# A retention and sparse-attention block on one core: the issue order of the second feed-forward's side work

## The chip, the core and the metric

The kernel runs on one core of a Trainium2 chip. The metric is the device time of one execution in microseconds (us), the median of the runs shown. The profile is one further execution, taken by the hardware profiler. PE is the matrix engine, PEld its weight loads, DVE the vector engine, ACT the scalar engine, POOL the general-purpose engine and SP the engine that only issues transfers; a "q" behind a name (SPq, ACTq) means the engine's instruction queue.

## The reference, cut to what matters

The block is a first feed-forward, a mixer (retention and index-selected attention) and a second feed-forward, then a final norm. The change touches only the last two lines:

```python
h = h + 0.5 * swiglu(rmsnorm(h, ffn1_norm), ...)
h = h + hybrid_mixer(rmsnorm(h, mix_norm), ...)
h = h + 0.5 * swiglu(rmsnorm(h, ffn2_norm), ffn2_w_gate, ffn2_w_up, ffn2_w_down)
y = rmsnorm(h, final_norm)          # [512 tokens, 1024], float32
# swiglu(u, wg, wu, wd) = (silu(u @ wg) * (u @ wu)) @ wd, with 2816 features
```

## The kernel before, in words

**Products of split numbers.** PE multiplies in a reduced float32 form. To keep float32 accuracy each operand is split in a high part (ACT copies it to the reduced type) and a low part (DVE subtracts the high part from the original): `in_two`, L323 for the high part and L324 for the low part. A product is then three matmuls, high·high, high·low and low·high. So every weight block costs ACT one high part and DVE one low part before PE can use it. `split` (L117, L118) does the same outside the step list.

**The step list.** The second feed-forward is a list of steps, walked by the generator `steps_through` (L328). Step i does, in program order: the loads of step i+4 (`pre`); the high part of the weights of step i+3 (two steps ahead at the very end); half of its own matmuls; then `lowers()`, the low part of those weights, and `catch_up()`, which runs whatever the list `late` holds; the other half of its matmuls; then its `posts`, side work for ACT and DVE. There are four weight buffers, so the high part of step i+3 has to wait until PE has left step i-1.

**The units.** The 2816 features come in six units, u0 to u5: u0 has 256 features, the others 512. u0 is computed plainly (`Plain`, four steps). Units u1 to u5 (`Rows`) use a seven-product scheme on halves of the tokens and of the inputs: 14 steps of 12 matmuls each (L2317), with sums and differences of weight quarters made by DVE (`wsum`, L2239). Three PSUM results X, Z, Y are made in turn; X lies in one PSUM area, Z and Y share another. ACT copies a result out (`copy`, L2258), DVE adds a second result to it (`add`, L2261), ACT takes silu of it (`silu`, L2266), DVE multiplies gate and up (`gated`, L2270) and turns the block for the next product (`turn`, L2277), POOL writes it to DRAM (`hts`, L2280), SP fetches it back in the other layout (`fetch`, L2287, one per token half: the half of room C first, then that of room D), and ACT and DVE split it again (`hidden`, the features hh and hl that the down product uses as stationary operand).

**Which side work goes where** is written out by hand in `posts_of` (L2560). For units u2 to u5: at step 3 `add("A", "Z")` and at once the silu of A; at step 11 `add("B", "Y")` and at once the silu of B; at steps 12 and 13 the two `gated` and `turn`. Since Y takes the PSUM area of Z, PE's step 6 has to wait for the add of Z at step 3. Since the next unit's X takes the area of X, its step 0 has to wait for `gated` of A.

**The down products** of the unit before (`down`, L2491, four steps of 24 matmuls, L2478) are woven in behind steps 7, 9, 11 and 13 of a unit (8 and 13 in u5). They are (output half c, features k0) = (0,0), (0,2), (1,0), (1,2). After the second step of a half, DVE adds its four PSUM blocks to the residual: `take`, put on `late`, so that it runs in the middle of the next step. For half c = 1 this next step is step 0 of the following unit. The adds are L2471 (four instructions), and L2464 for u0 (16 small ones a half).

**The end.** Behind u5's steps come u4's last two down steps, then u5's down for c = 0 in two steps (features 0 to 1 and 2 to 3, for token blocks b = 0, 1, 2, 3 in this order), then u5's c = 1 outside the step list, with the final norm (`finish`, `leave`). Token blocks 2 and 3 need half 1 of u5's features (room C), blocks 0 and 1 half 0 (room D). The weights of u5's c = 1 are one load of 1 MB (`load_w`, L133) into a buffer that held earlier down weights, split at L117 and L118. The gain of the final norm is loaded by ACT's queue at L2654.

**Who orders what.** Inside `manual_schedule(engines=BUSY)` PE, ACT and DVE issue in the order of the program; SP and POOL, and everything outside, are placed by the framework's planner, which fills a queue by its own estimate of what is ready when. All steps up to u4's second down step are in one such region, the last four steps in a second. Each engine's queue is strictly in order: an instruction that waits holds up those behind it.

Of the kernel before, what the change touches and what calls it, by code (L numbers as in the profile page):

```python
# [11 lines left out]
F32 = mybir.dt.float32  # L12
# [6 lines left out]
P = 128  # L19
D = 1024  # L20
KD = D // P
S = 512
# [59 lines left out]
def kernel(ctx: ExitStack, tc: tile.TileContext, x, meta, g1, wg1, wu1, wd1, gm,  # L82
                      w_in, w_ro, w_ao, w_mo, g2, wg2, wu2, wd2, gf, rope, decay, causal, out):
    nc = tc.nc
# [45 lines left out]
    def load_w(src, nk, n):  # L130
        raw = wpool.tile([P, 2048], F32, tag="raw", name="raw", bufs=2)
        v = raw[:, : nk * n].rearrange("p (k c) -> p k c", k=nk)
        nc.sync.dma_start(v, src.rearrange("(k p) c -> p k c", p=P))  # L133
        return v

    def split_w(v, eng=nc.vector):
        nk, n = v.shape[1], v.shape[2]
        hi = wpool.tile([P, 1024 + WPAD], F32R, tag="whi", name="whi", bufs=3)[:, w_at[0] :]
        lo = wpool.tile([P, 1024 + WPAD], F32R, tag="wlo", name="wlo", bufs=3)[:, w_at[0] :]
        hv = hi[:, : nk * n].rearrange("p (k c) -> p k c", k=nk)  # L140
        lv = lo[:, : nk * n].rearrange("p (k c) -> p k c", k=nk)
        split(v, hv, lv, eng)
        return hv, lv
# [226 lines left out]
    class Sevens:  # L370
# [50 lines left out]
        def gate_of(self, src, t, norm):  # L421

            nc.vector.tensor_tensor(t, src, norm, ALU.mult)
            nc.scalar.activation(t, t, AF.Silu)
            nc.vector.tensor_tensor(t, t, norm, ALU.mult)
            return t
# [23 lines left out]
        def split_t(self, n):  # L450
            split(self.ts[n], *self.tsum(n))
# [135 lines left out]
    if True:  # L587
# [120 lines left out]
        with tc.manual_schedule(engines={mybir.EngineType.PE, mybir.EngineType.Activation, mybir.EngineType.DVE}):  # L708
# [51 lines left out]
            def second_half(k):  # L760

                taken(second[k], 0)
                kept(second[k], False)
# [97 lines left out]
        def down(f0, nf, taken_by):  # L861

            raws = {}
            steps = []
            for c in range(KD):
                def pre(c=c):
                    if c % 2 == 0:
                        raws[c] = load_w(wd1[f0 * P : (f0 + nf) * P, c * P : (c + 2) * P], nf, 2 * P)

                def src(c=c):  # L870
                    return raws[c // 2 * 2][:, :, c % 2 * P : (c % 2 + 1) * P]

                def run(w, lower, c=c):
                    ps = [s1.bank("psd")[:, :TH] for _ in range(2)]
                    mm3([(ps[0], one), (ps[1], two)], w, lambda k: s1.hid[f0 + k], nf)
                    lower()
                    s1.catch_up()
                    for p_, sl in zip(ps, (one, two)):
                        nc.vector.scalar_tensor_tensor(hT[c][:, sl], p_, 0.5, hT[c][:, sl], ALU.mult, ALU.add)
                    taken_by(c)  # L880
                    s1.next_sum4()

                steps.append((pre, src, run))
            return steps
# [522 lines left out]
    if True:  # L1407
# [418 lines left out]
        p = RH - 1  # L1826
# [349 lines left out]
    TT, STT = nc.vector.tensor_tensor, nc.vector.scalar_tensor_tensor  # L2176
    xn = [hidp.tile([P, 4, S], F32, tag=f"h{c}", name="xn") for c in "hl"]
    one, two = slice(0, S // 2), slice(S // 2, S)
    late, f2 = [], {}

    def catch_up():

# [240 lines left out]
    def token_norm():  # L2423
        nc.vector.tensor_scalar(tok[:, 8:12], tok[:, :4], 1.0 / D, EPS, ALU.mult, ALU.add)
        nc.gpsimd.tensor_tensor(rcol, tok[:, 8:12], mhalf[:, :4], ALU.pow)

    def fetch_tokens():
        for b in range(4):
            nc.gpsimd.dma_start(hTok[b], hx[b * P : (b + 1) * P].rearrange("t h a e -> t (h a e)"))
# [58 lines left out]
            banks += [t[:, :S], t[:, S:]]  # L2488
        return banks

    def down(u, c, k0, banks, first=True, last=True, posts=(), taken_by=None, where=("d0", "d1"), held_last=False):  # L2491

        d = {}

        def pre():
            held = last_raw if held_last else down_raw
            if not held:
                t = wpool.tile([P, 2048], F32, tag="raw", name="raw", bufs=2).rearrange("p (h k c) -> p h k c", h=2, k=2)
                held.extend(t[:, i] for i in range(2))
            held.append(held.pop(0))  # L2500
            d["raw"] = held[-1]
            rows = slice((u.f0 + k0) * P, (u.f0 + k0 + 2) * P)
            nc.sync.dma_start(d["raw"], wd2[rows, c * S : (c + 1) * S].rearrange("(k p) c -> p k c", p=P))

        def run(w, lower):
            if k0 == 0 and first:
                banks.extend(new_down(where))
            for b in range(4):
                for k in range(2):
                    products([(banks[b], wide)], u, b, k0 + k, w, k, first and k0 + k == 0, last and k0 + k == u.nf - 1)  # L2510
                if b == 1:
                    lower()
                    catch_up()
            for do in posts:
                do()
            if last and k0 == u.nf - 2:
                def take():
                    for b in range(4):
                        add_sums(b, c, banks[b])
                        if taken_by:  # L2520
                            taken_by(b, c)
                if taken_by:
                    take()
                else:
                    late.append(take)

        return (pre, lambda: d["raw"], run, 0)

    fin = {}

    def finish(b, c):

# [27 lines left out]
    def posts_of(u):  # L2560

        i = u.i
        nxt = units[i + 1] if i + 1 < len(units) else None
        prev = units[i - 1] if i else None
        at = {j: [] for j in range(14)}

        def put(j, *do):
            at[j] += do

        gate_of = lambda c, half: lambda: u.silu(c, half)  # L2570
        if u is u0:
            put(0, lambda: split_t(1), lambda: new_t(2))
            put(1, lambda: split_t(2), lambda: new_t(3), lambda: squares(0))
            put(2, lambda: split_t(3), lambda: new_t(4), lambda: squares(1), lambda: squares(2), lambda: squares(3), token_norm)
            put(3, lambda: split_t(4), u.gates, lambda: u1.wsum(2, 0), lambda: late.append(u.turned))
            return at
        a, b = (4, 6) if u.early else (2, 4)
        put(a, lambda: prev.new_hidden(hid_tile), lambda: late.append(prev.hidden(1)))
        put(1, lambda: u.copy("A", "p1", "X"), lambda: u.wsum(2, 2))
        put(3, lambda: u.add("A", "Z"), gate_of("A", 0))  # L2580
        put(b, lambda: late.append(prev.hidden(0)))
        if not u.early:
            put(4, lambda: u.wsum(3, 0))
            put(5, lambda: u.wsum(3, 2))
        put(5, lambda: u.copy("B", "u2", "X"))
        put(6, lambda: u.wsum(4, 0))
        put(7, lambda: u.copy("C", "p5", "Y"), lambda: u.wsum(4, 2))
        put(9, lambda: u.add("C", "X"))
        put(11, lambda: u.add("B", "Y"), gate_of("B", 1))
        loads = {6: "21", 7: "11", 9: "12", 11: "22"}  # L2590
        put(12, lambda: u.gated("C", u.room["C"], u.room["B"], 1), lambda: u.turn("C", "D", 1), lambda: u.fetch("C", 1))
        put(13, lambda: u.gated("A", u.d["X"], u.room["A"], 0), lambda: late.append(turn_rest))

        def turn_rest():
            u.turn("A", "B", 0)
            u.fetch("D", 0)

        if nxt:
            for j, n in loads.items():
                put(j, lambda n=n: nxt.load(n))  # L2600
        return at
# [7 lines left out]
    def woven(i, places_):  # L2609

        for j, s in enumerate(wo[i]):
            steps.append(s)
            if j in places_:
                steps.append(places_[j])

    def downs(u, posts, **kw):
        banks = ([], [])
        return [down(u, c, k0, banks[c], posts=p, held_last=bool(kw and c and k0), **(kw if c else {}))
                for (c, k0), p in zip([(c, k0) for c in range(2) for k0 in range(0, u.nf, 2)], posts)]

    woven(1, dict(zip((9, 13), downs(u0, ((), sums_of(units[2]))))))
# [1 line left out]
        woven(i, dict(zip((7, 9, 11, 13), downs(units[i - 1], ((), (), (), sums_of(units[i + 1]))))))  # L2623
    u4, u5 = units[4:]

    def second_half():
        u5.new_hidden(last_tile)
        late.append(u5.hidden(1))

    d = downs(u4, ((), (), (second_half,), (lambda: u5.hidden(0)(),)), where=("x", "z"))  # L2630
    woven(5, {8: d[0], 13: d[1]})
    n_units = len(steps)
    c0, c1 = [], []
    steps += d[2:]
    steps.append(down(u5, 0, 0, c0, held_last=True))
    steps.append(down(u5, 0, 2, c0, taken_by=finish))
    pair = []

# [11 lines left out]
            next(pipe)  # L2650
    f2["later"].close()
    fp = fin["p"] = ctx.enter_context(pool("f2"))
    fin["gfb"] = fp.tile([P, D], F32, tag="gfb", name="gfb")
    nc.scalar.dma_start(fin["gfb"], gf.partition_broadcast(P))  # L2654
    fin["sums"] = fp.tile([P, 4, 16], F32, tag="sums", name="sums")
    fin["hg"] = [fp.tile([P, D], F32, tag=f"hg{b}", name=f"hg{b}") for b in range(4)]
    with tc.manual_schedule(engines=BUSY):
        for _ in pipe:
            pass
    raw = load_w(wd2[u5.f0 * P : (u5.f0 + 4) * P, S:], 4, 512)  # L2660
    ws = [split_w(raw[:, i : i + 2, :]) for i in (0, 2)]
    with tc.manual_schedule(engines=BUSY):
        part = slice(0, S // 2)
        c1 += new_down(("x", "z"))
# [57 lines left out]
```

## Time and profile before

| | |
|---|---|
| median of 3 runs (lowest to highest) | 1507.54 us (1506.84 to 1507.86) |
| the profiled execution: its time, its span | 1508.82 us, 1507.0 us |
| PE busy | 1486.2 us, 99% of the span |
| DVE, ACT, POOL busy | 75%, 47%, 11% |
| mean granted PE clock | 0.994 |
| second feed-forward | from 1150.3 us to the end |

How to read it: PE's busy time is the union of its matmuls, which overlap, so a short stop hides in it; the start times of matmuls in the timeline tell more. In the timeline a row is start, length, engine, line, operation, output<-inputs, count, and in brackets the idle time before it and what ended it. In the view of waits a row is engine, tile and line, what it waited for, and then total us, times and the longest.

### The profile page before, as it was taken

What the parts mean: (1) busy time and instruction counts of PE and PEld (TensorE: products, weight loads), DVE (VectorE), ACT (ScalarE), POOL (GpSimd) and SP (SyncE); (2) the same over time, 40 slices, a digit from 0 to 9 for tenths busy, and PEclk for the clock granted to TensorE, in tenths of its full rate; (3) what the DMA queues carried; (4) which work ended last, traced back from release to release, by engine and by line L of the source; (5) the groups of instructions that cost most, each with busy time, mean ns of one, the idle gap of its engine ahead of it and who ended that gap; (6) DMA issues with size and microseconds to landing.
All of it is one profiled execution on the core that took longest, in us unless ns stands there. A gap on an engine that the chain in (4) does not pass through costs nothing.

```text
span 1507.0 us, 22315 instructions
## 1 busy us (share of the span) xinstructions
PE 1486.2 (99%) x8848; PEld 1314.7 (87%) x8848; DVE 1125.1 (75%) x1715; ACT 714.5 (47%) x1028; POOL 159.8 (11%) x238
## 2 busy tenths in 40 slices
PE   9999999999999999999999999999999999999996
PEld 8999999999988888888898888988888878888875
DVE  4988585776886768678978778777567787876855
ACT  5655263454354444443334447667335634434433
POOL 1000000002111120100000032331003110110110
PEclk9999999999999999999999999999999999999997
DMA  5232333236644445231332335576466334354241
GB/s 170 60 119 90 111 100 113 85 99 187 219 146 171 168 139 166 94 122 60 128 101 72 110 97 167 158 199 186 154 225 201 106 119 167 113 167 146 78 151 59
DMA packets 160857, 200.54 MB, mean 133 GB/s; under 512 B 13680, under 2 KB 117256, under 8 KB 160112
## 3 DMA queue, kind: packets, MB, share of 16 engines
q1 hardware_dynamic: 146992, 162.53, 34.1%
q0 software_dynamic: 10080, 29.75, 6.0%
q10 hardware_dynamic: 3680, 6.84, 1.3%
q8 instruction: 69, 1.13, 0.3%
q14 instruction: 36, 0.29, 0.1%
HBM read 168.91 MB, written 30.16 MB: 132 GB/s over the span
## 4 chain that ended last, share of the span: by engine, by line
PE 90%; DVE 5%; issue 2%; ACT 2%; DMA 1%; POOLq 0%; POOL 0%; SPq 0%; DVEq 0%; ACTq 0%
PE psd L157 8%; PE psqX L157 7%; PE psd L2478 6%; PE psrg L157 6%; PE psro L157 6%; PE psqX L2317 5%; PE psvX L1181 4%; PE psqY L157 3%; PE psrk L157 3%; PE psrq L157 3%; PE psga L157 3%; PE psqY L2317 3%; PE psat L157 3%; PE psmo L157 3%; PE psak L157 3%; PE psaq L157 3%
## 5 line engine op out<-in xcount | busy, mean ns | idle before, releaser
L324 DVE TENSOR_TENSOR wlo<-raw,whi 128x1024 fp32r<-128x1024 f32 (+2 forms) x156 | 174.2, 1120 | 41.3 <-ACT whi L323 41.0
L323 ACT ACTIVATE whi<-raw 128x1024 fp32r<-128x1024 f32 (+2 forms) x156 | 147.6, 949 | 105.0 <-PE psd L157 37.5
L324 DVE TENSOR_TENSOR wlo<-w,whi 128x1024 fp32r<-128x1024 f32 x76 | 92.4, 1218 | 45.3 <-ACT whi L323 45.2
L323 ACT ACTIVATE whi<-w 128x1024 fp32r<-128x1024 f32 x76 | 80.1, 1058 | 97.0 <-PE psd L2478 31.2
L157 PE MATMUL psro<-vo,whi 128*128 128x512 f32 x256 | 78.9, 389 | 0.0
L117 ACT ACTIVATE whi<-raw 128x1024 fp32r<-128x1024 f32 (+1 forms) x44 | 45.4, 1036 | 55.6 <-PE psat L157 17.2
L118 DVE TENSOR_TENSOR wlo<-raw,whi 128x1024 fp32r<-128x1024 f32 (+1 forms) x44 | 53.7, 1220 | 23.6 <-ACT whi L117 23.5
L157 PE MATMUL psd<-hl,whi 128*128 128x264 f32 x352 | 71.2, 284 | 0.0
L157 PE MATMUL psd<-hh,wlo 128*128 128x264 f32 x352 | 70.9, 283 | 0.0
L157 PE MATMUL psd<-hh,whi 128*128 128x264 f32 x352 | 70.6, 282 | 0.0
L2478 PE MATMUL psd<-whi,hh 128*128 128x512 f32 (+1 forms) x148 | 58.2, 393 | 4.4 <-ACT hh L323 4.4
L157 PE MATMUL psqX<-th,whi 128*128 128x264 f32 x216 | 61.1, 283 | 0.0
L157 PE MATMUL psqX<-tl,whi 128*128 128x264 f32 x216 | 61.1, 283 | 0.0
L157 PE MATMUL psqX<-th,wlo 128*128 128x264 f32 x216 | 61.1, 283 | 0.0
L2478 PE MATMUL psd<-whi,hl 128*128 128x512 f32 (+1 forms) x148 | 58.2, 393 | 1.7 <-DVE hl L324 1.7
L2478 PE MATMUL psd<-wlo,hh 128*128 128x512 f32 (+1 forms) x148 | 58.1, 392 | 0.5 <-DVE wlo L324 0.5
L157 PEld LDWEIGHTS psro<-vo,whi 128*128 128x128 f32 x256 | 48.1, 188 | 10.2
L157 PEld LDWEIGHTS psd<-hh,wlo 128*128 128x128 f32 x352 | 54.4, 188 | 0.0
L157 PEld LDWEIGHTS psd<-hh,whi 128*128 128x128 f32 x352 | 54.3, 188 | 0.0
L157 PEld LDWEIGHTS psd<-hl,whi 128*128 128x128 f32 x352 | 53.9, 188 | 0.0
L323 ACT ACTIVATE whi<-wsum 128x1024 fp32r<-128x1024 f32 x36 | 38.1, 1059 | 30.3 <-PE psd L157 14.8
L2280 POOL DMA_DIRECT2D hts<-cross x40 | 25.7, 649 | 249.9 <-DVE cross L2277 249.2
(579 smaller groups left out, 4678.4 us busy)
## 6 DMA issues: line engine op xcount, KB each, us to landing
raw<-in_w_in_dram SPq DMA_DIRECT2D x18, 1024.0 KB, 5.4
raw<-in_w_in_dram SPq DMA_DIRECT2D x33, 512.0 KB, 4.0
raw<-in_ffn_w_down_dram SPq DMA_DIRECT2D x24, 512.0 KB, 3.9
w<-in_w_in_dram SPq DMA_DIRECT2D x24, 512.0 KB, 6.2
raw<-in_ffn_w_up_dram SPq DMA_DIRECT2D x11, 1024.0 KB, 5.1
raw<-in_ffn_w_gate_dram SPq DMA_DIRECT2D x10, 1024.0 KB, 5.1
w<-in_ffn_w_up_dram SPq DMA_DIRECT2D x20, 512.0 KB, 4.2
w<-in_ffn_w_gate_dram SPq DMA_DIRECT2D x20, 512.0 KB, 5.4
```

Source lines behind the costliest of these rows:

```text
L117: nc.scalar.activation(hi, src, AF.Copy)
L118: eng.tensor_tensor(lo, src, hi.bitcast(F32), ALU.subtract)
L157: nc.tensor.matmul(o, a[:, k, :], b[:, sl], start=first and k == 0 and i == 0, stop=last and k == nk - 1 and i == 2, skip_group_check=onto)
L323: nc.scalar.activation(hi, src, AF.Copy)
L324: return lambda: nc.vector.tensor_tensor(lo, src, hi.bitcast(F32), ALU.subtract)
L1181: nc.tensor.matmul(d[bank_][t], a, b[:, k, :], start=not onto and j + k + m == 0, stop=j + k == 3 and m == 2, skip_group_check=onto)
L2280: nc.gpsimd.dma_start(d.rearrange("(b i) a e -> a i b e", i=32)[a], cross[32 * a : 32 * a + 32].rearrange("p b c t -> p b (c t)"))
L2317: nc.tensor.matmul(ps[:, t], a, b[:, k, :], start=not onto and j + k + m == 0, stop=j + k == 3 and m == 2, skip_group_check=onto)
L2478: nc.tensor.matmul(ps, a, m[:, j, cs], start=first and i == 0, stop=last and i == 2)
```

## The change

Seven edits, all in the second feed-forward:

1. The silu of A and of B are no longer issued behind their add in `posts`, but put on `late`: they run in the middle of the next step, behind the high part that this step issues.
2. The adds (`take`) of a unit's half c = 1 go on a list of their own, `put_off`, for u0 to u3, and run in `posts` of step 2 of the next unit instead of the middle of step 0. For u4 they stay on `late`.
3. u5's features: half 1 was split (high part in `posts` of u4's third down step, low part in the middle of the fourth) and half 0 in `posts` of the fourth. Now both high parts and then both low parts stand in `posts` of the fourth (`last_halves`).
4. u5's first down step takes the token blocks in the order 2, 3, 0, 1.
5. The load and the splits of the weights for u5's c = 1 move from behind the step list into `posts` of u5's first down step (`tail_weights`).
6. The second region orders SP as well.
7. The gain of the final norm is loaded by SP during u0's step 3, into a part of `RR` that u0's squares used until then, and not by ACT's queue at the end.

```diff
+    def load_gf():
+        fin["gfb"] = RR[:, :D]
+        nc.sync.dma_start(fin["gfb"], gf.partition_broadcast(P))
...
-    def down(u, c, k0, banks, ..., held_last=False):
+    def down(u, c, k0, banks, ..., held_last=False, put_off=late, rows=range(4)):
...
-            for b in range(4):
+            for i, b in enumerate(rows):
...
-                    late.append(take)
+                    put_off.append(take)
...
-            put(3, lambda: split_t(4), u.gates, lambda: u1.wsum(2, 0), lambda: late.append(u.turned))
+            put(3, load_gf, lambda: split_t(4), u.gates, lambda: u1.wsum(2, 0), lambda: late.append(u.turned))
...
-        put(3, lambda: u.add("A", "Z"), gate_of("A", 0))
+        put(2, lambda: put_off and put_off.pop()())
+        put(3, lambda: u.add("A", "Z"), lambda: late.append(gate_of("A", 0)))
...
-        put(11, lambda: u.add("B", "Y"), gate_of("B", 1))
+        put(11, lambda: u.add("B", "Y"), lambda: late.append(gate_of("B", 1)))
...
+    put_off = []
     def downs(u, posts, **kw):
         banks = ([], [])
+        kw = kw or {"put_off": put_off}
...
-    def second_half():
-        u5.new_hidden(last_tile)
-        late.append(u5.hidden(1))
-    d = downs(u4, ((), (), (second_half,), (lambda: u5.hidden(0)(),)), where=("x", "z"))
+    def last_halves():
+        u5.new_hidden(last_tile)
+        lows = [u5.hidden(half) for half in (1, 0)]
+        for low in lows:
+            low()
+    def tail_weights():
+        raw = load_w(wd2[u5.f0 * P : (u5.f0 + 4) * P, S:], 4, 512)
+        tail_w.extend(split_w(raw[:, i : i + 2, :]) for i in (0, 2))
+    d = downs(u4, ((), (), (), (last_halves,)), where=("x", "z"))
...
-    steps.append(down(u5, 0, 0, c0, held_last=True))
+    steps.append(down(u5, 0, 0, c0, held_last=True, posts=(tail_weights,), rows=(2, 3, 0, 1)))
...
-    fin["gfb"] = fp.tile([P, D], F32, tag="gfb", name="gfb")
-    nc.scalar.dma_start(fin["gfb"], gf.partition_broadcast(P))
...
-    with tc.manual_schedule(engines=BUSY):
+    with tc.manual_schedule(engines=BUSY | {mybir.EngineType.SP}):
         for _ in pipe:
             pass
-    raw = load_w(wd2[u5.f0 * P : (u5.f0 + 4) * P, S:], 4, 512)
-    ws = [split_w(raw[:, i : i + 2, :]) for i in (0, 2)]
+    ws = tail_w
```

More of the change, by code (lines that the diff above doesn't have):

```diff
@@ L2178 @@
     one, two = slice(0, S // 2), slice(S // 2, S)
-    late, f2 = [], {}
+    late, f2, fin = [], {}, {}
     def catch_up():
@@ L2489, in new_down, with down @@
         return banks
-    def down(u, c, k0, banks, first=True, last=True, posts=(), taken_by=None, where=("d0", "d1"), held_last=False):
+    def down(u, c, k0, banks, first=True, last=True, posts=(), taken_by=None, where=("d0", "d1"), held_last=False, put_off=late, rows=range(4)):
         d = {}
@@ L2507, in run @@
                 banks.extend(new_down(where))
-            for b in range(4):
+            for i, b in enumerate(rows):
                 for k in range(2):
                     products([(banks[b], wide)], u, b, k0 + k, w, k, first and k0 + k == 0, last and k0 + k == u.nf - 1)
-                if b == 1:
+                if i == 1:
                     lower()
@@ L2524, in run @@
                 else:
-                    late.append(take)
+                    put_off.append(take)
         return (pre, lambda: d["raw"], run, 0)
-    fin = {}
     def finish(b, c):
@@ L2614, in woven @@
                 steps.append(places_[j])
+    put_off = []
     def downs(u, posts, **kw):
         banks = ([], [])
-        return [down(u, c, k0, banks[c], posts=p, held_last=bool(kw and c and k0), **(kw if c else {}))
+        kw = kw or {"put_off": put_off}
+        return [down(u, c, k0, banks[c], posts=p, held_last=bool("where" in kw and c and k0), **(kw if c else {}))
                 for (c, k0), p in zip([(c, k0) for c in range(2) for k0 in range(0, u.nf, 2)], posts)]
@@ L2624 @@
     u4, u5 = units[4:]
-    def second_half():
+    tail_w = []
+    def last_halves():
         u5.new_hidden(last_tile)
-        late.append(u5.hidden(1))
-    d = downs(u4, ((), (), (second_half,), (lambda: u5.hidden(0)(),)), where=("x", "z"))
+        lows = [u5.hidden(half) for half in (1, 0)]
[5 more added lines that the diff above has]
+    d = downs(u4, ((), (), (), (last_halves,)), where=("x", "z"))
     woven(5, {8: d[0], 13: d[1]})
```

## The prediction

> **What bounds the kernel now.** I read the page first (PE busy 99% of the span), then PE's waits from 1150 us on, where the second feed-forward begins.
>
> ```profile
> PE psd L2478 <- ACT hh L323: 4.4, 1, 4.4
> PE psqY L2317 <- DVE p L2261: 1.8, 1, 1.8
> PE psd L2478 <- DVE hl L324: 1.7, 2, 1.4
> ```
>
> PE bounds the stage; what a reordering can win is what PE loses in a few stops. Busy time hides part of them, so I measured starts in the timeline. Undisturbed, a step of 24 matmuls takes 5.44 us, one matmul 0.227:
>
> ```profile
> 1264.78 5.44 PE psqY L2317 x24
> ```
>
> At the end, the last matmul of u4's fourth down step, the first four of u5's, and the one at which the pace is normal again:
>
> ```profile
> 1466.56 0.39 PE L2478 MATMUL psd<-whi,hl 128*128 128x512 f32 x1
> 1471.32 0.80 PE L2478 MATMUL psd<-whi,hh 128*128 128x512 f32 x1 [4.37 <-ACT hh L323]
> 1471.91 0.63 PE L2478 MATMUL psd<-wlo,hh 128*128 128x512 f32 x1
> 1473.91 0.80 PE L2478 MATMUL psd<-whi,hl 128*128 128x512 f32 x1 [1.36 <-DVE hl L324]
> ...
> 1479.96 0.39 PE L2478 MATMUL psd<-wlo,hh 128*128 128x512 f32 x1
> ```
>
> The third matmul was due at 1466.56 + 3 x 0.227 = 1467.24 and started at 1473.91, 6.67 late. The 14 intervals to 1479.96 took 6.05 instead of 3.17, 2.88 more. Together 9.55 us. The slow matmuls are a clock matter: the view by windows has the granted clock (the number behind POOL's) at 0.83 here.
>
> ```profile
> 1467.00:1498.00 31.00, 25.32 (x106) 20.62 (x107) 18.54 (x30) 10.39 (x19) 1.30 (x2) 0.83 0.07 23
> ```
>
> [...]
>
> In u2 (its first matmul, its step 6, and the step behind the first down step):
>
> ```profile
> 1221.25 0.39 PE L2478 MATMUL psd<-whi,hl 128*128 128x512 f32 x1
> 1222.30 0.47 PE L2317 MATMUL psqX<-whi,xh 128*128 128x512 f32 x1 [0.66 <-DVE p L2270]
> ...
> 1239.55 0.39 PE L2317 MATMUL psqX<-wlo,th 128*128 128x512 f32 x1
> 1241.70 0.47 PE L2317 MATMUL psqY<-wpair,th 128*128 128x512 f32 x1 [1.77 <-DVE p L2261]
> ...
> 1253.73 0.39 PE L2317 MATMUL psqX<-whi,th 128*128 128x512 f32 x1
> ```
>
> From 1221.25 to 1253.73 there are 121 intervals: 27.43 us due, 32.48 taken, 5.05 lost, of which 0.82 at the first stop and 1.92 at the second. Two small stops remain, in u1 (0.2) and in u5 at u4's first down step (0.87 - 0.23 = 0.64, and 0.1 for the next matmul: 0.75).
>
> ```profile
> 1191.43 0.39 PE L2317 MATMUL psqY<-whi,tl 128*128 128x512 f32 x1
> 1191.84 0.50 PE L2317 MATMUL psqY<-wlo,th 128*128 128x512 f32 x1
> ...
> 1430.63 0.39 PE L2478 MATMUL psd<-whi,hh 128*128 128x512 f32 x1
> 1431.50 0.50 PE L2478 MATMUL psd<-wlo,hh 128*128 128x512 f32 x1 [0.48 <-DVE wlo L324]
> ```
>
> So at most 0.2 + 5.05 + 0.75 + 9.55 = 15.55 us can be won. The change removes no instruction from PE, DVE or ACT.
>
> **Silus behind the next high parts.** The cause of the stops in u1, u2 and u5 is one pattern. DVE, the end of u1 and the start of u2, and ACT's silu:
>
> ```profile
> 1211.26 1.22 DVE L324 TENSOR_TENSOR wlo<-raw,whi 128x1024 fp32r<-128x1024 f32 x1
> 1212.39 1.22 DVE L2261 TENSOR_TENSOR u<-psqY,u 128x1024 f32<-128x1024 f32 x1
> 1215.96 1.23 DVE L324 TENSOR_TENSOR wlo<-w,whi 128x1024 fp32r<-128x1024 f32 x1 [2.35 <-ACT whi L323]
> ...
> 1228.93 3.69 DVE L2464 SCALAR_TENSOR_TENSOR hTok<-psd,hTok 128x128 f32<-128x128 f32 x16
> ...
> 1236.08 1.23 DVE L324 TENSOR_TENSOR wlo<-w,whi 128x1024 fp32r<-128x1024 f32 x1 [1.19 <-ACT whi L323]
> ...
> 1240.34 1.22 DVE L2261 TENSOR_TENSOR p<-psqZ,p 128x1024 f32<-128x1024 f32 x1
> ```
> ```profile
> 1213.64 1.34 ACT L2266 ACTIVATE u<-u,RR 128x512 f32<-128x512 f32 x2 [4.73 <-DVE u L2261]
> ```
>
> The add releases the silu; the next high part stands behind the silu on ACT, and DVE idles 2.35 us for it. With the change that high part (whose buffer PE has left by then) is done while ACT waited anyway, and DVE goes on at 1212.39 + 1.13 = 1213.5. What waits for the silu itself, `gated`, comes one instruction later, at 1214.65, with the first silu done by 1214.36 and the second by 1214.98: no new wait over 0.3. Behind the silu on ACT now stands only what stood behind that high part. So DVE is 2.4 us earlier at every silu. In u1 that exceeds the 0.2 lost, and in u5 the 0.64: both stops go. At the start of u2, `gated` of A, whose end let PE go at 1222.30, is done by 1219.9, ahead of 1221.25 + 0.23 = 1221.48 where PE wants X: 0.9 goes.
>
> **Adds two steps later.** In u2, DVE reaches the place of the adds at 1228.93 - 2.4 = 1226.5. Now come the low part of step 4 (1.3 with its high part, which needs the sum just made), a weight sum (1.13), the 1.19 of waiting for that sum's high part, the low part of step 5 (1.13): 1231.2. Then the adds (3.7): 1234.9, a low part and half 1's low part (2 x 1.13), the add of Z (1.22): 1238.4, and 0.14 later PE's step 6 (before: 1241.56 to 1241.70). PE wants it at 1221.48 + 6 x 2.72 = 1237.8. So 0.7 remains, 0.8 with the restart: 4.25 of 5.05 is won. Between the ends (DVE not ahead at all: 2 us stay; the adds fill every wait: 0) I take the sum. The features' low part for half 0 is ready 0.2 before PE's third down matmul; if not, 0.3 is lost.
>
> In u3 to u5 nothing waited at Z. u5's adds and its add of Z, and PE's step 6:
>
> ```profile
> 1409.48 2.47 DVE L2471 SCALAR_TENSOR_TENSOR hTok<-psd,hTok 128x512 f32<-128x512 f32 x4
> ...
> 1419.67 1.22 DVE L2261 TENSOR_TENSOR p<-psqZ,p 128x1024 f32<-128x1024 f32 x1
> ```
> ```profile
> 1422.37 0.39 PE L2317 MATMUL psqY<-whi,th 128*128 128x512 f32 x1
> ```
>
> The add ends at 1420.9, 1.5 ahead of PE, with the same instructions before it in either order: 0. If a wait of DVE that the adds filled now opens elsewhere, the worst is 2.47 - 1.5 = 1.0 a unit.
>
> **The end.** The queue of SP, POOL's writes for half 0, and ACT:
>
> ```profile
> 1445.22 5.21 SPq L2503 DMA_DIRECT2D raw<-in_ffn_w_down_dram  x3
> 1458.48 0.37 SPq L133 DMA_DIRECT2D raw<-in_ffn_w_down_dram  x1
> 1459.03 7.75 SPq L2287 DMA_DIRECT2D land<-hts  x2
> ```
> ```profile
> 1457.64 2.57 POOL L2280 DMA_DIRECT2D hts<-cross  x4 [2.20 <-DVE cross L2277]
> ```
> ```profile
> 1467.13 1.12 ACT L323 ACTIVATE hh<-land 128x1024 fp32r<-128x1024 f32 x1 [9.96 <-DMA land<-hts]
> 1468.14 1.05 ACT L323 ACTIVATE whi<-raw 128x1024 fp32r<-128x1024 f32 x1
> ```
> ```profile
> land<-hts SPq DMA_DIRECT2D x10, 512.0 KB, 3.9
> ...
> raw<-in_ffn_w_down_dram SPq DMA_DIRECT2D x1, 1024.0 KB, 6.5
> ```
>
> The 1 MB tail load stands ahead of both feature fetches although the program issues it last. It waits from 1450.4 to 1458.48 for its buffer (the low part ending there). Half 1 is issued behind it, takes 8.1 instead of 3.9, and on ACT holds the weights' high part (1468.14) behind it. After: the weights' high and low parts no longer stand behind it (PE leaves the needed buffer 5.44 before the step's end, at 1461.4: done by 1463.8), and PE wants first half 1, then, 12 matmuls later, half 0.
>
> Does the tail load move behind the fetches? SP is ordered in the second region alone, where the tail load is its only instruction; the fetches are issued in the first. Nothing in the diff ties the two, so I take the old order as likeliest. Then half 1 lands at 1467.1 as before (end a), or some 1.5 earlier, as POOL's writes, some 2 earlier by the silu, are mostly through before the 1 MB starts (end b). Its high part ends 1.1 later, its low part 1.2 after that: 1469.4 or 1467.9, against 1467.24: 2.2 or 0.7 lost; I take 1.4. Half 0's writes ended issuing at 1460.2, and SP fetched at 1459.03 + 7.75 - 0.37 = 1466.4, 6.2 later; 2 earlier, that is 1464.4 at the latest. At 3.9 it lands by 1468.3, its low part is done by 1470.6; PE wants it at 1469.4 + 10 x 0.227 = 1471.7 (end a), or at 1470.2 (end b), where it lands earlier too: 0. The stops are then under 2 us, and such a stop (1.77 at 1241.70) did not lower the clock. 9.55 - 1.4 = 8.15 won. The second half of the tail weights gets its buffer as u5's first down step ends and takes 2.3 to split; PE asks 5.44 later: 0, and one for one beyond 3.1; on ACT only `finish` stands behind them.
>
> **The gain's load** goes into SP's queue at u0's step 3 and waits there for the last of four squares, which ends at 1167.7 + 1.06 = 1168.8. The squares, and SP's next row:
>
> ```profile
> L2421 ACT ACTIVATE RR<-hTok x4: 1055/1064/1065, 1161.2 to 1167.7; 128x1024 f32<-128x1024 f32 x4
> ```
> ```profile
> 1183.83 3.65 SPq L2386 DMA_DIRECT2D land<-hts  x2
> ```
>
> Nothing is due on SP until 1183.83: 0. Without those 15 us the fetch there would be held for as long as the load waits.
>
> **Sum.** 0.2 + 4.25 + 0.75 + 8.15 = 13.35 us. Span 1507.0 - 13.35 = 1493.65. The profiled execution took 1508.82, 1.3 over the median of the runs, 1507.54; against this median: 1494.2 us. Behind the last matmul nothing changes.
>
> **Rivals.** (1) SP's order is put right: half 1 lands long before PE asks, and half 0 by the 1468.3 above or earlier, its low part by 1470.6, where PE, now undisturbed, wants it at 1467.24 + 12 x 0.227 = 1469.96. 9.55 or all but 0.6 of it goes: 1492.8 to 1493.4. For it: `gated` some 2 earlier may let the planner find half 1's fetch ready before the tail load's buffer. Against: the order shown above. 28%.
>
> (2) The old order, and SP's transfers in series: half 1 lands at 1458.48 + 6.5 + 3.9 = 1468.9, the low part at 1471.2, 4.0 lost, with a slow clock up to 6.9: 1496.8 to 1499.7. Against: before, the same pair landed at 1467.1. 10%. [...]
>
> (3) u2 keeps its stop: the adds now lie close ahead of the add of Z, and any delay of a high part there counts in full. The stop at Z stays at 2.0 instead of 0.8, that at X at 0.9: 2.1 less, 1496.3. 10%.
>
> (4) The edits do little of what they say: the end keeps its 9.55 (half 0 lands as late as before) and u2 its 5.05; 0.95 is won, 1506.6, within 0.2%. 4%.
>
> (5) Slower: the planner fills SP's queue anew, and a hold like the one at 1450.4 (8.1 us) gets ahead of half 0's fetch in u2 to u5. Half 0's fetch before u5:
>
> ```profile
> 1405.35 7.74 SPq L2287 DMA_DIRECT2D land<-hts  x2
> ```
>
> It is issued at 1412.7, lands at 1416.6 and is split in 2.3; PE wants the low part at 1430.63 + 0.45 = 1431.1. So the hold decides only from 12 us on; at 16.5 it costs four times 4.5 = 18: 1512. No row shows more than 8.1. 3%.
>
> The forecast has the remaining 45%.
>
> **How the numbers follow.** 0.2% is 3 us, about what a measurement of this kernel can tell: faster by more means under 1504.5. Forecast and rivals 1 to 3 are all there: 0.93; same 0.04, slower 0.03. Range: low 1491.5 (all 15.55 won, and 0.5 of jitter), high 1499 (rival 2 nearly whole); rivals 4 and 5 stay out.
>
> **What would show it.** Right: no 2.35 us idle of DVE on a high part behind an add; X of u2 without a wait; PE's wait for p L2261 under 1; no window with the clock at 0.83 before the last 15 us. SP's timeline tells forecast from rival 1: L133 ahead of or behind L2287. Wrong: PE's wait for hh or hl above 3 us, new waits for p L2261 in u3 to u5, or a span above 1500.

## The result and the profile after

The changed kernel takes 1493.59 us (median of 5 runs, 1491.80 to 1494.11), the one before 1507.54 beside it (5 runs, 1505.99 to 1507.98): a ratio of 0.9907, with a 95% interval of 0.9892 to 0.9921. The forecast was 1494.2. The profiled execution has a span of 1491.8 us and a mean granted clock of 0.998 (before: 1507.0 and 0.994). In the code of after, the matmuls of the down products are L2482, the loads of their weights L2507, the adds L2468 and L2475; the other lines that the prediction names are unchanged.

PE's waits from 1150 us to the last matmuls, where a row is engine, tile and line, what was waited for, then total us, times and the longest:

```profile
PE psqY L2317 <- DVE p L2261: 0.5, 1, 0.5
PE psd L2482 <- DVE hl L324: 0.5, 1, 0.5
PE psd L2482 <- ACT hh L323: 0.4, 1, 0.4
```

Of the 4.4 and the 1.8 us, about half a microsecond each is left. The first wait is step 6 of u2, the other two are u5's down product. PE's starts there (start, length, engine, line, operation, tiles, and in brackets the idle time):

```profile
1235.90 0.39 PE L2317 MATMUL psqX<-wlo,th 128*128 128x512 f32 x1
1236.83 0.47 PE L2317 MATMUL psqY<-wpair,th 128*128 128x512 f32 x1 [0.54 <-DVE p L2261]
1237.14 0.39 PE L2317 MATMUL psqY<-wpair,tl 128*128 128x512 f32 x1
...
1459.72 0.39 PE L2482 MATMUL psd<-whi,hl 128*128 128x512 f32 x1
1460.49 0.50 PE L2482 MATMUL psd<-whi,hh 128*128 128x512 f32 x1 [0.38 <-ACT hh L323]
1460.83 0.39 PE L2482 MATMUL psd<-wlo,hh 128*128 128x512 f32 x1
1461.75 0.50 PE L2482 MATMUL psd<-whi,hl 128*128 128x512 f32 x1 [0.53 <-DVE hl L324]
1462.09 0.39 PE L2482 MATMUL psd<-whi,hh 128*128 128x512 f32 x1
```

An undisturbed interval between two starts is 0.227. Step 6 begins 1236.83 - 1235.90 - 0.227 = 0.70 late, and the next matmul 0.08. At the end the four intervals are 0.54, 0.11, 0.69 and 0.11 too long, 1.45 together. In this document "lost" is this sum, the excess over 0.227, over all intervals longer than 0.30 us in the second feed-forward of the profiled execution: 15.42 us before (0.30 in u1, 4.82 in u2, 0.76 in u5, 9.54 at the end), 2.23 after (0.78 in u2, 1.45 at the end). 13.19 us of the gain stand in these intervals.

DVE at the end of u1 and in u2, and ACT's silu at the same place:

```profile
1210.72 1.22 DVE L2261 TENSOR_TENSOR u<-psqY,u 128x1024 f32<-128x1024 f32 x1
1211.86 1.22 DVE L324 TENSOR_TENSOR wlo<-w,whi 128x1024 fp32r<-128x1024 f32 x1
1212.99 1.41 DVE L2270 SCALAR_TENSOR_TENSOR p<-p,RR,u 128x512 f32<-128x512 f32 x2
...
1216.64 1.40 DVE L2270 SCALAR_TENSOR_TENSOR p<-psqX,RR,p 128x512 f32<-128x512 f32 x2
...
1229.65 3.62 DVE L2468 SCALAR_TENSOR_TENSOR hTok<-psd,hTok 128x128 f32<-128x128 f32 x16
...
1235.47 1.22 DVE L2261 TENSOR_TENSOR p<-psqZ,p 128x1024 f32<-128x1024 f32 x1
```
```profile
1211.97 1.34 ACT L2266 ACTIVATE u<-u,RR 128x512 f32<-128x512 f32 x2 [2.01 <-DVE u L2261]
1213.22 1.04 ACT L323 ACTIVATE whi<-w 128x1024 fp32r<-128x1024 f32 x1
```

No row shown behind the add has an idle time: the 2.35 us are gone here. `gated` of A ends at 1218.04 and the next X starts, unhindered, at 1219.81. The add of Z ends at 1236.69, and PE's step 6 starts 0.14 later: DVE still ends that wait, 0.70 late.

SP, ACT and DVE at the end:

```profile
1438.38 2.76 SPq L2507 DMA_DIRECT2D raw<-in_ffn_w_down_dram  x3
1451.62 0.37 SPq L133 DMA_DIRECT2D raw<-in_ffn_w_down_dram  x1
1452.16 1.36 SPq L2287 DMA_DIRECT2D land<-hts  x2
```
```profile
1454.71 1.06 ACT L323 ACTIVATE whi<-raw 128x1024 fp32r<-128x1024 f32 x1 [4.38 <-PE psd L2482]
1459.32 1.12 ACT L323 ACTIVATE hh<-land 128x1024 fp32r<-128x1024 f32 x1 [3.55 <-DMA land<-hts]
1460.63 1.17 ACT L323 ACTIVATE hh<-land 128x1024 fp32r<-128x1024 f32 x1 [0.19 <-DMA land<-hts]
```
```profile
1460.47 2.58 DVE L324 TENSOR_TENSOR hl<-land,hh 128x1024 fp32r<-128x1024 f32 x2 [3.44 <-ACT hh L323]
```

The tail load (L133) still stands ahead of both feature fetches (L2287). The weights' high part no longer stands behind the features' (1454.71 against 1459.32), and the second fetch is issued 1.0 us behind the first, where it took 7.4 before. In the view by windows the granted clock is 1.00 from 1455 to 1475; before, the matmuls of this place were 0.43 us apart, with 0.66 granted from 1466 to 1481:

```profile
1455.00:1475.00 20.00, 19.09 (x83) 15.21 (x82) 13.22 (x19) 7.25 (x11) 0.00 (x0) 1.00 0.21 75
```

### The profile page after: what moved, and what is told of

Its sections match the earlier page's. It is cut to its first block, busy times and chain, and to the rows that moved or that the text cites. A ratio compares the mean times of both kernels' runs of the same rounds, so it can differ in the third digit from the quotient of the medians.

```text
span 1491.8 us, 22317 instructions
## 1 busy us (share of the span) xinstructions
PE 1479.4 (99%) x8848; PEld 1313.5 (88%) x8848; DVE 1125.4 (75%) x1715; ACT 716.2 (48%) x1028; POOL 159.9 (11%) x238
## 5 line engine op out<-in xcount | busy, mean ns | idle before, releaser
L2482 PE MATMUL psd<-whi,hl 128*128 128x512 f32 (+1 forms) x148 | 56.8, 384 | 0.5 <-DVE hl L324 0.5
L2482 PE MATMUL psd<-whi,hh 128*128 128x512 f32 (+1 forms) x148 | 56.8, 384 | 0.4 <-ACT hh L323 0.4
L2482 PE MATMUL psd<-wlo,hh 128*128 128x512 f32 (+1 forms) x148 | 56.7, 383 | 0.0
```

Source lines behind the costliest of these rows:

```text
L2482: nc.tensor.matmul(ps, a, m[:, j, cs], start=first and i == 0, stop=last and i == 2)
```

## The experiments

The theory: every stop has its own cause, and each edit takes away its own. The silu behind the high part (edit 1) frees DVE in u1, u2 and u5; the adds (edit 2) are worth something only when DVE is ahead; the end is won by edits 3 to 5, and what stays there is the tail load ahead of the fetches. The rivals: the end alone makes the gain; the adds alone held up u2; the ordering of SP or the gain's load matters. In the table "lost" is the sum as above, in the profiled execution.

| kernel | median (range, runs), us | ratio to before, 95% | lost, us |
|---|---|---|---|
| s_silu: before with edit 1 | 1501.00 (1500.16 to 1501.66, 4) | 0.9957 [0.9941, 0.9974] | 8.50 |
| s_adds: before with edit 2 | 1506.86 (1505.70 to 1508.18, 10) | 1.0000 [0.9991, 1.0010] | 14.21 |
| s_end: before with edits 3 to 7 | 1500.50 (1499.54 to 1502.04, 4) | 0.9957 [0.9942, 0.9971] | 8.44 |
| a_sp_gf: after without edits 6, 7 | 1493.64 (1493.31 to 1494.39, 4) | 0.9911 [0.9896, 0.9926] | 1.28 |
| a_rows: after without edit 4 | 1494.36 (1493.36 to 1494.85, 4) | 0.9916 [0.9901, 0.9930] | 2.44 |
| a_split: after without edit 3 | 1496.35 (1495.51 to 1497.61, 4) | 0.9928 [0.9911, 0.9944] | 5.56 |
| b_order: tail load behind the fetches | 1492.68 (1492.32 to 1492.87, 4) | 0.9905 [0.9890, 0.9920] | 0.78 |
| r_after: after, unaltered | 1493.41 (1492.08 to 1493.84, 4) | 0.9905 [0.9889, 0.9922] | 1.61 |
| b_adds: adds behind the add of Z | 1492.67 (1492.06 to 1493.44, 4) | 0.9902 [0.9888, 0.9917] | 1.05 |
| b_both: b_order and b_adds | 1491.70 (1491.52 to 1491.78, 4) | 0.9899 [0.9884, 0.9913] | 0.21 |

**The silu alone.** On the kernel before:

```diff
-        put(3, lambda: u.add("A", "Z"), gate_of("A", 0))
+        put(3, lambda: u.add("A", "Z"), lambda: late.append(gate_of("A", 0)))
-        put(11, lambda: u.add("B", "Y"), gate_of("B", 1))
+        put(11, lambda: u.add("B", "Y"), lambda: late.append(gate_of("B", 1)))
```

> Before, with edit 1 alone (silus behind the next high parts). Theory (each edit takes away its own stop): u1's 0.2, u5's 0.75 and u2's stop at X (0.9) go; at u2's step 6 DVE is 2.4 earlier but still has the adds at step 0, so about 1.5 is lost there; the end keeps most of its stop, because half 1's fetch still stands behind the tail load and ACT is still held by it, perhaps 0.9 less, as the writes of half 0 are out of the way earlier. About 5.3 us faster: 1502.2. Rival (the end alone makes the gain, the silu's order is hidden by PE): within 1 us of before.

6.0 us faster than the 1507.04 beside it. The stops in u1, u5 and at X are gone; Z keeps 1.53, so the units lose 4.35 less. The end loses 6.97 instead of 9.54, which goes past the expectation. SP's two fetches are now issued together, although no line of the end was edited.

```profile
1453.88 0.37 SPq L133 DMA_DIRECT2D raw<-in_ffn_w_down_dram  x1
1454.42 1.36 SPq L2287 DMA_DIRECT2D land<-hts  x2
```

Before, half 0's fetch waited for POOL's writes until 1466.4. The DMA view of that stretch gives KB each and median us from issue to landing, first of before, then of s_silu (one write of half 1 among its five):

```profile
raw<-in_ffn_w_down_dram SPq DMA_DIRECT2D x1, 1024.0 KB, 6.5
land<-hts SPq DMA_DIRECT2D x2, 512.0 KB, 5.9
hts<-cross POOLq DMA_DIRECT2D x4, 128.0 KB, 6.6
```
```profile
hts<-cross POOLq DMA_DIRECT2D x5, 128.0 KB, 2.7
```

Before, POOL began to issue half 0's writes at 1457.64, with the tail load following at 1458.48. The first write landed after 2.4 us, the other three after 6.4 to 6.8. In s_silu POOL begins at 1450.62, 3.3 ahead of the tail load instead of 0.8, and the median of its row is 2.7 instead of 6.6.

Not all of the difference at the end, 2.57 us, is due to this. Behind the second stop the starts stayed about 0.43 apart for 3.89 us here and for 6.05 before. s_adds below, whose end is not edited either, loses 8.25 there. So the 9.54 of before is the figure of one execution, and another with the same end lost 1.3 less.

**The adds alone.** On the kernel before:

```diff
-                    late.append(take)
+                    put_off.append(take)
...
+        put(2, lambda: put_off and put_off.pop()())
```

> Before, with edit 2 alone (adds of half c = 1 at step 2 of the next unit). Theory: without the lead of the silus it only moves the low part of step 5 ahead of the adds: u2's stop of 0.79 there goes, the one at X stays and PE's step 6 waits about 2.4, 0.6 us faster in all: 1506.9. Rival (the adds were what held up u2): u2's 5.05 goes by more than half, 1504.5 or less.

Nothing that can be measured: 1506.86 against 1507.04, where 0.6 was expected. Step 5 of u2 no longer stops, but the add of Z comes that much later, PE's stop there is longer, and u2 loses 4.82 as before. The run shows something of the clock. s_adds, then s_end, which stops at the same place:

```profile
1237.70 0.39 PE L2317 MATMUL psqX<-wlo,th 128*128 128x512 f32 x1
1240.16 0.52 PE L2317 MATMUL psqY<-wpair,th 128*128 128x512 f32 x1 [2.08 <-DVE p L2261]
1240.48 0.63 PE L2317 MATMUL psqY<-wpair,tl 128*128 128x512 f32 x1
1240.91 1.05 PE L2317 MATMUL psqY<-wpair,th 128*128 128x512 f32 x2
```
```profile
1237.82 0.40 PE L2317 MATMUL psqX<-wlo,th 128*128 128x512 f32 x1
1239.97 0.47 PE L2317 MATMUL psqY<-wpair,th 128*128 128x512 f32 x1 [1.75 <-DVE p L2261]
1240.27 0.39 PE L2317 MATMUL psqY<-wpair,tl 128*128 128x512 f32 x1
```

After 2.08 us of idling the starts are 0.43 apart from the second interval on; after 1.75 the first interval is 0.30, and those behind it are 0.23. The windows around the two stops (the number behind POOL's is the granted clock):

```profile
1237.00:1245.00 8.00, 5.92 (x19) 4.44 (x18) 5.65 (x6) 4.95 (x6) 0.00 (x0) 0.79 0.00 0
```
```profile
1236.50:1244.50 8.00, 6.20 (x27) 4.47 (x26) 5.64 (x6) 4.64 (x6) 0.00 (x0) 1.00 0.00 0
```

**The end alone.** The changed kernel with edits 1 and 2 taken back:

```diff
-        put(3, lambda: u.add("A", "Z"), lambda: late.append(gate_of("A", 0)))
+        put(3, lambda: u.add("A", "Z"), gate_of("A", 0))
-        put(11, lambda: u.add("B", "Y"), lambda: late.append(gate_of("B", 1)))
+        put(11, lambda: u.add("B", "Y"), gate_of("B", 1))
...
-        kw = kw or {"put_off": put_off}
```

> Edits 3 to 7 without 1 and 2 (silus and adds as before). Theory: u1, u2 and u5 lose their 6.0 as before. At the end half 0 is written 2 us later than with the silus' lead, so its low part is late as well: about 2.5 lost there instead of 9.55, 7.0 us faster: 1500.5. Rival (the end alone makes the gain): 1493.6 to 1495.

6.5 us faster than before. The units lose 5.59, nearly what they lost before, and the end 2.85 instead of 9.54. So the end alone does not make the gain. The stops at X (0.90) and in u5 (0.79) are there as before; the one in u1 is not, although the silus stand where they stood before. Half 0's fetch stands for POOL's writes again, which it does not with the silu:

```profile
1456.78 0.37 SPq L133 DMA_DIRECT2D raw<-in_ffn_w_down_dram  x1
1457.33 7.88 SPq L2287 DMA_DIRECT2D land<-hts  x2
```

The three groups of edits alone give 6.0 + 0.2 + 6.5 = 12.7; together they give 13.95. The difference lies within the intervals of the times. By the traces the end loses 2.85 with its own edits and 1.45 with the silu too, and the adds win only behind the silu (1.53 at Z becomes 0.78).

**Without the ordering of SP and the gain's load on it.**

```diff
-            put(3, load_gf, lambda: split_t(4), ...
+            put(3, lambda: split_t(4), ...
...
-    with tc.manual_schedule(engines=BUSY | {mybir.EngineType.SP}):
+    with tc.manual_schedule(engines=BUSY):
```

> The changed kernel with edits 6 and 7 undone (SP not ordered in the second region, the gain of the final norm loaded by ACT's queue at the end). Theory: neither does anything, 1493.6, the tail load ahead of both fetches, and PE losing about 1.5 at the end and 0.8 at u2's step 6. Rival (ordering SP, or taking the transfer off ACT's queue, made part of the end's gain): half 1 lands later or the weights' high part is held, 1 us or more lost there besides.

1493.64: these two edits are worth nothing that can be measured here. SP's rows stand in the same order as in after. Yet this profile loses only 0.19 at the end, not 1.45; that is taken up under "the changed kernel once more". It also loses 0.30 in u1, at another step than before did, where after loses nothing.

**The old order of token blocks.**

```diff
-... posts=(tail_weights,), rows=(2, 3, 0, 1)))
+... posts=(tail_weights,)))
```

> The changed kernel with the token blocks of u5's first down step in the order 0, 1, 2, 3 again. Theory: PE then needs half 0 first, whose high part ended 1.3 and whose low part 1.3 after half 1's: the first matmul waits until 1461.85, the third until 1463.1 instead of 1461.75: 1.3 us more lost, 2.8 in all: 1494.9. Rival (the order of the blocks is what took away the end's stop): 4 us or more lost and a low clock, 1499 or more.

1494.36, 0.8 more than after, but the ranges overlap and after was not measured beside it, so the times do not show that the order of the blocks is worth anything. In the trace the end loses 1.66.

**The features split as before.**

```diff
-    def last_halves():
+    def second_half():
         u5.new_hidden(last_tile)
-        lows = [u5.hidden(half) for half in (1, 0)]
-        for low in lows:
-            low()
+        late.append(u5.hidden(1))
...
-    d = downs(u4, ((), (), (), (last_halves,)), where=("x", "z"))
+    d = downs(u4, ((), (), (second_half,), (lambda: u5.hidden(0)(),)), where=("x", "z"))
```

> The changed kernel with edit 3 undone (half 1's high part issued by ACT ahead of the next weights' high part again, the block order 2, 3, 0, 1 kept). Theory: ACT waits for half 1 with the weights' high part behind it, whose low part then stands ahead of half 1's on DVE: half 1's low part ends at about 1463.9 instead of 1461.7, 2.2 us more lost: 1495.8. Rival (the splits' place does nothing, only the block order does): 1493.6.

1496.35, 2.8 more than after. ACT's and PE's rows:

```profile
1459.70 1.12 ACT L323 ACTIVATE hh<-land 128x1024 fp32r<-128x1024 f32 x1 [8.69 <-DMA land<-hts]
1460.72 1.05 ACT L323 ACTIVATE whi<-raw 128x1024 fp32r<-128x1024 f32 x1
1461.67 1.12 ACT L323 ACTIVATE hh<-land 128x1024 fp32r<-128x1024 f32 x1
```
```profile
1461.21 0.39 PE L2482 MATMUL psd<-wlo,hh 128*128 128x512 f32 x1
1464.21 0.80 PE L2482 MATMUL psd<-whi,hl 128*128 128x512 f32 x1 [2.61 <-DVE hl L324]
1464.81 0.63 PE L2482 MATMUL psd<-whi,hh 128*128 128x512 f32 x1
1465.23 0.63 PE L2482 MATMUL psd<-wlo,hh 128*128 128x512 f32 x1
```

The weights' high part, which after does at 1454.71, stands on ACT behind half 1's and so waits for its landing, and DVE does the weights' low part (from 1461.80) ahead of half 1's (from 1462.94). PE idles 2.61, the starts behind it are 0.43 apart for 3.5 us, and the granted clock is 0.83 from 1460 to 1470, which the expectation had not priced.

**The tail load behind the fetches.** On the changed kernel, with the planner told that the load follows half 0's fetch:

```diff
-        raw = load_w(wd2[u5.f0 * P : (u5.f0 + 4) * P, S:], 4, 512)
+        with tc.issue_after(u5.fetched.ins):
+            raw = load_w(wd2[u5.f0 * P : (u5.f0 + 4) * P, S:], 4, 512)
```

> The changed kernel with the tail load queued behind half 0's fetch on SP (the order that rival 1 of the prediction had). Theory: half 1 is fetched at about 1448.5 and lands by 1453, half 0 at about 1454 and lands by 1459; PE does not wait at the end; the 1.5 lost there go: 1492.1. Rival (the transfers are not held by the tail load but by DRAM or by POOL's writes, or PE's stop only moves to the tail weights): as the changed kernel, 1493.6, or slower.

```profile
1449.61 5.85 SPq L2287 DMA_DIRECT2D land<-hts  x2
1455.57 0.45 SPq L133 DMA_DIRECT2D raw<-in_ffn_w_down_dram  x1
```

The order is turned round, and no stop is left at the end: the loss there came with the tail load's place. Its price in time is less certain. The median is 0.9 under after's, but the two were not measured side by side, the ranges overlap, and the ratios to the kernel before (0.9905 and 0.9907) hardly differ.

**This, and the adds behind the add of Z.**

```diff
-        put(2, lambda: put_off and put_off.pop()())
-        put(3, lambda: u.add("A", "Z"), lambda: late.append(gate_of("A", 0)))
+        put(3, lambda: u.add("A", "Z"), lambda: put_off and put_off.pop()(), lambda: late.append(gate_of("A", 0)))
```

> As the run before, and the adds of half c = 1 behind the add of Z at step 3. Theory: the add of Z in u2 no longer has 3.7 us of adds ahead of it, PE's step 6 does not wait, another 0.8 goes, and the next low part, 3.7 later, is still ahead of its step: 1491.3, PE without a stop over 0.2 from 1150 on. Rival (DVE is at its limit in u2, so the stop moves to step 7 or to the down step behind it): 0.8 or more lost there, 1492.1 or slower.

1491.70: its slowest run (1491.78) lies below every run of b_order beside it (from 1492.32) and, narrowly, below every run of after (from 1491.80). PE has no wait left in the view of waits; 0.21 is lost at u2's first down step, whose third matmul waits for the low part of half 0. DVE's rows, the add of Z now ahead of the adds:

```profile
1232.91 1.22 DVE L2261 TENSOR_TENSOR p<-psqZ,p 128x1024 f32<-128x1024 f32 x1
1234.05 3.62 DVE L2468 SCALAR_TENSOR_TENSOR hTok<-psd,hTok 128x128 f32<-128x128 f32 x16
```

The add ends at 1234.13, and PE takes step 6 without a stop at 1236.27.

**The changed kernel once more, and the adds alone.**

> The changed kernel once more, unaltered, for its profile. My theory: how long the 1 MB tail load and the two feature fetches behind it take differs by about 1 us from one execution to the next, and that alone decides whether PE stops at the end. The tail load took 6.3 us in the changed kernel's profile (1.5 us of PE lost at the end), 5.1 with edits 6 and 7 undone (nothing lost) and 5.2 with the old block order (1.7 lost). Then this run has the tail load between 5.0 and 6.5 us and a loss at the end between 0 and 1.5 us that goes with it: near 0 if it is under 5.4. Rival: edits 6 and 7 themselves cost the 1.1 us (another queue order or a busier memory); then the tail load takes 6.3 again and the loss at the end is 1.5 again. Time 1493.6 by both.

The tail load's row in the list of DMA issues, in after, r_after and a_sp_gf, all with the same order on SP:

```profile
raw<-in_ffn_w_down_dram SPq DMA_DIRECT2D x1, 1024.0 KB, 6.3
```
```profile
raw<-in_ffn_w_down_dram SPq DMA_DIRECT2D x1, 1024.0 KB, 5.7
```
```profile
raw<-in_ffn_w_down_dram SPq DMA_DIRECT2D x1, 1024.0 KB, 5.1
```

The end loses 1.45, 0.81 and 0.19. The same kernel thus has two different tail loads and losses, and the loss follows the load; the rival's 6.3 and 1.5 did not come again. b_adds, with this end too, fits in: 5.7 and 0.81. In a_rows the load took 5.2, with which the new block order would have lost little, going by the 5.1 and 0.19 of a_sp_gf; it lost 1.66, since block 0 asks at once for half 0, which lands last. What makes the load take longer or shorter, these runs do not show.

b_adds is the changed kernel with the last diff alone, the tail load staying ahead of the fetches.

> The changed kernel with the adds of a unit's half c = 1 behind the add of Z at step 3 instead of ahead of it at step 2; the tail load stays ahead of the fetches. My theory: PE's step 6 in u2 no longer waits for the add of Z, so the 0.79 us lost there goes and nothing else changes: 1492.8, and together with the tail load's 0.9 that is the 1.9 us that both edits won. Rival: the two edits need each other, and the adds alone win nothing (1493.6) or put a new wait in front of PE's next X (over 1494).

1492.67, 0.74 under the 1493.41 of the unaltered kernel beside it, with ranges that overlap. The profile has no wait for the add of Z any more. That the adds' place is worth about this much is also seen from b_both, 0.98 under b_order beside it, with ranges that do not overlap. With b_order's 0.9 the 0.74 make 1.65 of b_both's 1.9. This agrees with two edits that add up, but times so close do not prove it.

## Why the prediction was right

The time (1494.2 against 1493.59) and the mechanism held in the main. By its own steps:

**u1, X of u2, u5.** Forecast 0.2, 0.9 and 0.75 won. All three stops are gone, in s_silu too, where nothing but the silu was moved. X and u5 stop as before in s_adds (0.90, 0.68) and s_end (0.90, 0.79), where it was not moved: these two were the silu's. For u1 that is not shown: its stop is gone in s_end as well, and a_sp_gf, with the silu moved, has one of 0.30 there.

That DVE is 2.4 us earlier "at every silu" holds only near it. At the end of u2 DVE waited 2.35 and 1.47 us for high parts before (rows at 1274.14 and 1276.84); after, it waits 3.92 at once (1270.89), and the ends of u3 and u4 look the same. The lead pays where a result of DVE that comes out ahead of that wait lets PE go on.

**Z of u2.** Forecast 0.8 left: 0.70 + 0.08 = 0.78. The add of Z ends where the sum over DVE's instructions from the silu on had put it: 1238.4 - 1221.48 = 16.9 us behind the start of X, measured 1236.69 - 1219.81 = 16.88. s_silu leaves 1.53 there and s_adds more than before, so the small rest needs both edits. That the adds fill DVE's place just ahead of the add of Z, as rival 3 has it, is true, but costs only this 0.78, and b_adds wins it.

**u3 to u5, and the gain's load.** Forecast 0 for both. The view of waits has p L2261 once, in u2, and a_sp_gf measures no difference.

**The end.** Forecast 1.4 left, the middle between its two cases of 2.2 and 0.7: 1.45 in the one profile and 0.81 in the other. The late part was half 1's, as forecast; half 0 came in time. The case called end b, where the writes get through first and half 1 lands some 1.5 earlier, was the right one. Behind the tail load's issue half 1 landed after 8.6 us before, after 7.1 in r_after and b_adds, which lost 0.81, and after 7.7 in after's profile, where the load itself was slower. That the middle of two cases fell on the 1.45 is luck. So is part of the start of the sum: the 9.55 at the end held 6.05 us of starts about 0.43 apart, and s_adds lost 1.3 less there.

One step had the wrong picture. The prediction took the 6.2 us between POOL's last issue and half 0's fetch as something that the edits only shift by 2. Three of the four writes took 6.4 to 6.8 us beside the tail load and half 1's fetch before; in after, where they are issued ahead of both, all took 2.4 to 2.8, so half 0's fetch followed half 1's by 1.0 us. The end did not turn on this: half 0 then landed 7.5 us after its issue instead of 3.7, and was split from 1.3 us behind half 1 on, in time for PE.

**The rivals.** SP's order was not put right (rival 1), and put right by hand it gave 1492.68, just under the 1492.8 to 1493.4 forecast for it. Transfers in series (rival 2) would have had half 1 land 6.5 + 3.9 = 10.4 us behind the tail load's issue; it was 1459.32 - 1451.62 = 7.7. The load took 6.3 and half 1's fetch, issued 0.5 behind it, 7.1, so the two overlapped. Rivals 4 and 5 left no trace: no hold on SP in u2 to u5 reached PE.

**The size.** The sum was 13.35; the intervals show 13.19, the medians 13.95, whose interval reaches from 0.0079 to 0.0108 of 1507.54, 11.9 to 16.3 us. The 0.8 between intervals and medians lies within that. The spans of the two profiles differ by more, 15.2: 13.77 lie between the first matmul of u1 (1172.02 before, 1170.85 after) and the last (1498.16, 1483.22), and 1.17 ahead of u1.

## What to carry to other kernels

Lay the starts of the bound engine's instructions against their undisturbed pace: here a sum over some thirty intervals told nearly the whole gain, while the share of busy time (99% before and after) told nothing. Where a queue keeps the order of the program, put an instruction that waits for a neighbour's fresh result behind one that is ready (on ACT the weights' high part ran at 1460.72 behind half 1's in a_split, at 1454.71 ahead of it in after); but moving work to a later place pays only if the thing that waits stands ahead of it there, as b_adds against s_adds shows. A large load that nobody needed yet went here with slower small transfers on both sides of it: those issued behind it on its queue (half 0's fetch took 7.5 us behind the tail load in after, 3.9 ahead of it in b_order), and the writes beside it (6.4 to 6.8 us for three of four before, 2.4 to 2.8 ahead of it in after).

## What the runs showed of the hardware

**Behind idle times of 2.08, 2.61 and 2.72 us the matmuls were slower, behind 1.75 and 1.77 us they were not.** Idle times of 2.08 (s_adds, granted clock 0.79 in the window around it), 2.61 (a_split, 0.83) and 2.72 (s_silu) were followed by starts 0.43 apart; 1.75 (s_end, 1.00) and 1.77 (before, 1.00 from 1200 to 1250) were not. Behind the first two, which no second stop followed, this lasted 3.7 and 3.5 us (1240.16 to 1243.88 in s_adds, where nine intervals took 1.6 us more than behind the stop at the full clock in s_end); behind the second of two stops it took 6.05 in before and 3.89 in s_silu. Whether the length alone decides, or also where the stop falls, these cases do not tell.

**The same transfer differed by 1.2 us.** The 1 MB tail load took 5.1 to 6.3 us in profiles with the same order on its queue (a_sp_gf 5.1, after 6.3), and 6.3 and 5.7 in two executions of the same program (after, r_after).

**Writes beside the tail load took more than twice as long as writes ahead of it.** Three of POOL's four writes of 128 KB took 6.4 to 6.8 us next to the tail load and half 1's fetch in before, and all four 2.4 to 2.8 ahead of both in after. In s_end half 0's fetch, which waits for them, was issued about 6.9 us behind the last of them.
